# The seam between a normed product and the next sublayer, with its three engines in written order

## The chip, the cores and the metric

The kernel runs on one core of one Trainium2 chip. The metric is the time of one execution in device microseconds (us); several executions of each kernel are compared. The engines are called TensorE (PE), VectorE (DVE), ScalarE (ACT), GpSimd (POOL) and SyncE (SP, which issues the loads).

## What is computed

Two stacks of transformer layers on a sequence of 256 tokens of width 1024, in float32. Each of the two layers of the first stack is a mixer, a cross-attention and an mlp; the second stack, two layers more, has a mixer and a gated feed-forward in each. What matters here is the seam between two sublayers of the first stack: a product, the norm of what it gives, the sum into x, and the norm of the new x, which is what the next product reads.

```python
def rms_norm(x, g):
    xf = x.astype(jnp.float32)
    y = xf * lax.rsqrt(jnp.mean(xf * xf, axis=-1, keepdims=True) + RMS_EPS)
    return (y * g.astype(jnp.float32)).astype(x.dtype)
...
        x = x + rms_norm(merged @ w_mix_out[l], ln_mix_post[l])

        h = rms_norm(x, ln_xa_pre[l])
        mn = rms_norm(mem, ln_mem[l])
        x = x + rms_norm(cross_attention(h, mn, xa_wq[l], xa_wkv[l], xa_wo[l]), ln_xa_post[l])

        h = rms_norm(x, ln_mlp_pre[l])
        x = x + rms_norm(jnp.square(jax.nn.relu(h @ mlp_w1[l])) @ mlp_w2[l], ln_mlp_post[l])
```

## The kernel before

**Layout.** x is held with its 1024 features as eight chunks of 128 partitions by 256 tokens. A weight block of 128 output features is a piece of 128x1024. A product of float32 accuracy is three products of rounded parts: each operand is split into a high part and the rest, and hi·hi, hi·lo and lo·hi are added in PSUM. So a block costs 8 (chunks) x 3 = 24 matmuls of 128x256.

**Weights.** Pieces are loaded by SP into `wraw`. `Weights.make` splits one: ACT copies it into `whi` (L371), DVE subtracts that into `wlo` (L372). There are four buffers of each, and `Weights.get` keeps three pieces made ahead of the one in use.

**The end of a normed product** (`post_units`, `post_evict`, `post_close`). There are three such products in a layer of the first stack: "mo" (the mixer's output), "xo" (the cross-attention's output) and the second product of the mlp. For each of eight output blocks, ACT squares the block out of PSUM (`ysq`, L698), ACT or DVE scales it into `yg` (L701, L703), and DVE adds the squares up in `yacc` (L707). After the last block `inv_rms` takes the mean over features with matmuls of 128x1 (from `yacc` and the last `ysq`), DVE adds epsilon (`st_m`, L461), POOL takes the power -1/2 (`st_tm_y`, L451), and PE spreads the result over the partitions in PSUM (`rp`). Then yg is multiplied by it and added to x: for the first two chunks one by one on DVE (L716, L719), for the next two in one go (L724), for the last four on POOL (L726), from a copy of rp in SBUF that ACT makes (`st_rep_y`, L717).

**The start of the next sublayer.** The new x, times the gain of the next norm, is split into `xgh` (ACT, L508) and `xgl` (DVE, L509), chunk by chunk. The factor 1/rms of this norm is taken out of the product and put in behind it, so the product can start before it is known. For that factor ACT squares x two chunks at a time (`sq_acc`, L493, then `sq_t`, L496, three times, through one buffer), and POOL adds them up (three adds of 128x512, L497, and one of 128x256, L500). `opening` runs the first three blocks of the product side by side, chunk by chunk, since chunk k of x becomes known one after the other. The mean over `sq_acc` stands in PE's order behind these three blocks and a fourth, that is behind 96 matmuls.

**What sets the order.** In the part of the program that is touched here a list scheduler sets the order of the instructions on each engine from its own estimates. Only from a later phase on the code is run with `manual_schedule`, in which PE, ACT and DVE follow the order in which the code is written. POOL and SP are never fixed that way.

Of the kernel before, what the change touches and what calls it, by code (L numbers as in the profile page):

```python
# [307 lines left out]
class Weights:  # L308


    def __init__(self, nc, w, ring, parts, tails, keys, ahead):
        self.nc, self.w, self.ring, self.parts, self.tails = nc, w, ring, parts, tails
        self.subs = []
        off, _ = _offsets()
        for key in keys:
            for i in range(len(off[key][1])):
                self.subs.append((key, i))
        self.ahead = ahead
        self.made, self.used = 0, 0
        self.ready = []  # L320
        self.keys, self.sent, self.loaded = keys, 0, deque()

    def deepen(self, open_pool, n):

# [24 lines left out]
        self.loaded.append(([t[:, j * m : j * m + m] for j in range(n)], tail))  # L349

    def make(self):
        nc = self.nc
# [8 lines left out]
        res = []  # L361
        for tail in range(1 + (subs[i] > 1024)):
            src = self.curt[:, i, :] if tail else self.cur[i]
            pool, bufs, n = (self.tails, 2, 256) if tail else (self.parts, 4, min(subs[i], 1024))
            tag = "t" if tail else "m"
            hi = pool.tile([P, 256 if tail else 1024], F32R, name="whi", tag="whi" + tag, bufs=bufs)
            lo = pool.tile([P, 256 if tail else 1024], F32R, name="wlo", tag="wlo" + tag, bufs=bufs)
            step = n if 0 < self.made < len(self.subs) - 2 else 512
            for g in range(0, n, step):
                c = slice(g, g + step)  # L370
                nc.scalar.activation(hi[:, c], src[:, c], AF.Copy)  # L371
                nc.vector.tensor_sub(lo[:, c], src[:, c], hi[:, c].bitcast(F32))  # L372
            res += [hi, lo]
        self.ready.append((key, i, *res))
        self.made += 1

    def get(self, key, i):
        while self.made < len(self.subs) and self.made <= self.used + self.ahead:
            self.make()
        k, j, *res = self.ready.pop(0)  # L380
        assert (k, j) == (key, i), ((k, j), (key, i))
        self.used += 1
        return res


class Net:
    def __init__(self, tc, io, out, ctx, tap=None, stop=None):
        self.tc, self.nc, self.io, self.out, self.ctx = tc, tc.nc, io, out, ctx
        self.tap = tap or (lambda name, ap: None)
        self.stop = stop  # L390
# [62 lines left out]
    def inv_rms(self, parts, tag):  # L453

        nc = self.nc
        ps = self.bank()
        for h in range(2):
            for i, sq in enumerate(parts):
                self.mm(ps[:, h : h + 1], sq[:, h * P : h * P + P], self.cv("mean"), i == 0, i == len(parts) - 1)
        m = self.keep.tile([P, 2], F32, name="st_m", tag="st_m", bufs=2)  # L460
        nc.vector.tensor_scalar(m, ps[:, 0:2], EPS, None, op0=ALU.add)  # L461
        tm = self.keep.tile([P, 2], F32, name="st_tm_" + tag, tag="st_tm_" + tag)
        self.rsqrt(tm, m, 2)
        return tm
# [79 lines left out]
    def order(self):  # L544

        self.ordered = self.tc.manual_schedule(engines=ORDERED)
        self.ordered.__enter__()

    def run(self, units):

        for u in units:
            if u[0] == "w":
                u[3](*self.ws.get(u[1], u[2]))
            else:
                u[1]()
# [16 lines left out]
    def fm_units(self, key, xh, xl, evict, nblk=2, each=False):  # L572

        st = {}

        def begin(i):
            if i == 0 or each:
                st["ps"] = self.bank("mm")
            return part(i)

        def part(i):
            o = 0 if each else i * S
            return st["ps"][:, o : o + S]
# [7 lines left out]
        def step(i, k, hi, lo):  # L591
            a, b = (xh(), xl()) if callable(xh) else (xh, xl)
            self.lin_k(part(i), hi, lo, a, b, k, k == 0 and i == 0, k == 7, skip_group_check=True)
# [12 lines left out]
    @staticmethod  # L606
    def ramp(units, n=3):

        held, out, count = [], [], 0
        for u in units:  # L610
            if u[0] != "w" or count == n:
                out.append(u)
                continue
            count += 1

            def g(hi, lo, parts=u[3].parts, last=count == n):
                held.append((parts, hi, lo))
                if not last:
                    return
                for (begin, _, _, i), _, _ in held:  # L620
                    begin(i)
                for k in range(8):
                    for (_, step, _, i), h, l in held:
                        step(i, k, h, l)
                for (_, _, end, i), _, _ in held:
                    end(i)

            out.append((*u[:3], g))
        return out

    def opening(self, units, n=3, a=3, held=4, b=4):
# [3 lines left out]
        for u in units:  # L635
# [3 lines left out]
            if count < held:  # L639
                begin, step, end, i = u[3].parts  # L640
                ends.append((end, i))

                def g(hi, lo, p=u[3].parts, at=count):
                    side.append((p, hi, lo))
                    if at < n - 1:
                        return
                    for (begin, _, _, i), _, _ in side:
                        begin(i)
                    for k in range(8):
                        for (_, step, _, i), h, l in side:  # L650
                            step(i, k, h, l)
                    side.clear()

                out[-1] = (*u[:3], g)
            if count == a:
# [25 lines left out]
    def post_units(self, kind, l, xh, xl, gkey, nxt):  # L681
# [2 lines left out]
        units = []  # L684
        for j in range(4):
            units += self.fm_units((kind, l, j), xh, xl, lambda i, ps, j=j: self.post_evict(2 * j + i, ps, gkey, l), each=True)
        units.append(("x", lambda: self.post_close(nxt)))
        return units

    def post_evict(self, n, ps, gkey, l):  # L690
        nc = self.nc
        if n == 0:
            self.yg = self.keep.tile([P, 8, S], F32, name="yg", tag="big")
            self.yacc = self.keep.tile([P, S], F32, name="yacc", tag="sq_acc")
            sq = self.yacc
# [4 lines left out]
        if n % 2 == 0:  # L700
            nc.scalar.activation(self.yg[:, n, :], ps, AF.Copy, scale=g)  # L701
        else:
            nc.vector.tensor_scalar(self.yg[:, n, :], ps, g, None, op0=ALU.mult)  # L703
        if n == 7:
            self.ylast = sq
        elif n > 0:
            nc.vector.tensor_add(self.yacc, self.yacc, sq)  # L707

    def post_close(self, nxt):
        nc = self.nc  # L710
        rp, _ = self.stat([self.yacc, self.ylast], "y", copy=False)
        rep = self.early.tile([P, S], F32, name="st_rep_y", tag="st_rep_y")
        self.prep(nxt)
        yg, x = self.yg, self.x
        for c in range(2):
            nc.vector.tensor_mul(yg[:, c, :], yg[:, c, :], rp)  # L716
        nc.scalar.activation(rep, rp, AF.Copy)  # L717
        for c in range(2):
            nc.vector.tensor_add(x[:, c, :], x[:, c, :], yg[:, c, :])  # L719
        self.prep_pair(0)  # L720
        for j in range(1, 4):
            v = yg[:, 2 * j : 2 * j + 2, :]
            if j == 1:
# [3 lines left out]
        for j in range(1, 4):  # L727
            v, xv = yg[:, 2 * j : 2 * j + 2, :], x[:, 2 * j : 2 * j + 2, :]
            nc.vector.tensor_add(xv, xv, v)
            self.prep_pair(j)  # L730


    def softmax(self, s, nh, n, pool, gate=None, stride=None):
# [95 lines left out]
    def mix_phase(self, l):  # L829
# [7 lines left out]
        def open_c():  # L837
# [6 lines left out]
            nc.gpsimd.memset(st["zr"][:, :, 0:1], 0.0)  # L844
# [841 lines left out]
    def mlp_phase(self, l):  # L1686
# [27 lines left out]
        units += second(14) + second(15)  # L1714

        def close():
            self.post_close(("ln_mix_pre", 1) if l == 0 else ("nmix", 0))
# [49 lines left out]
    def even_phase(self):  # L1767
# [3 lines left out]
        def pre():  # L1771
# [5 lines left out]
            nc.gpsimd.memset(st["xr"][:, :, 0:3], 0.0)  # L1777
# [936 lines left out]
```

## Time and profile before

| what | us |
|---|---|
| runs shown | 2707.53, 2710.4, 2711.75 |
| their median | 2710.4 |
| the profiled execution | 2709.63 |
| its span, first to last instruction | 2707.8 |
| PE busy | 2643.1 (98%) |
| DVE busy | 2068.0 (76%) |
| ACT busy | 1601.1 (59%) |
| POOL busy | 213.5 (8%) |

The span is the part of an execution between its first and its last instruction. An engine's busy time counts its instructions alone, so the span less PE's busy time is the time in which PE did nothing. The granted clock is a share of full speed: 1.00 is 2.4 GHz and 0.50 is 1.2 GHz.

### The profile page before, as it was taken

The numbers are of one execution on the slowest core, as the hardware profiler recorded it, in microseconds if no ns is written. First come the engines' busy times: TensorE is split into PE (matmuls) and PEld (weight loads), VectorE is DVE, ScalarE is ACT, GpSimd is POOL, SyncE is SP. The second block draws the span as 40 slices with busy tenths as digits, with TensorE's granted clock in tenths as the row PEclk, the third lists the DMA queues.
The fourth block names the chain that finished last, engine by engine and source line by source line (L and its number), as shares of the span: only waits on it lengthen the run. The fifth ranks groups of instructions, "written<-read, shape, count | busy, mean of one in ns | idle before, by whom it ended". The sixth has DMA issues, their size and how long they took to land.

```text
span 2707.8 us, 44209 instructions
## 1 busy us (share of the span) xinstructions
PE 2643.1 (98%) x17870; PEld 2405.5 (89%) x17870; DVE 2068.0 (76%) x2527; ACT 1601.1 (59%) x2136; POOL 213.5 (8%) x188
## 2 busy tenths in 40 slices
PE   8999999999999999999999999999999999999998
PEld 7989999998989999998999999778887888788876
DVE  6776756556875765557876677999999999999997
ACT  4434545444533544444654456777777777777776
POOL 1031101001031111001010011000000000000000
PEclk9999999999999999999899999999999999999999
DMA  7423444553322433554375544999899989998991
GB/s 255 138 98 134 156 156 169 185 187 137 133 100 98 179 141 140 180 180 163 118 297 186 179 175 175 354 358 364 321 363 356 365 323 363 354 357 333 359 353 66
DMA packets 99853, 612.70 MB, mean 226 GB/s; under 512 B 10616, under 2 KB 20344, under 8 KB 31928
## 3 DMA queue, kind: packets, MB, share of 16 engines
q1 hardware_dynamic: 99208, 608.74, 60.9%
q8 instruction: 142, 2.33, 0.3%
q0 software_dynamic: 432, 1.06, 0.1%
q14 instruction: 71, 0.58, 0.1%
HBM read 608.17 MB, written 1.06 MB: 225 GB/s over the span
## 4 chain that ended last, share of the span: by engine, by line
PE 49%; DVE 2%; ACT 1%; issue 0%; POOL 0%; ACTq 0%
PE ps_mm L422 32%; PE ps_b L422 16%; PE ps_b L426 1%; DVE wlo L372 1%; ACT whi L371 0%; DVE room L430 0%; DVE mt L2280 0%; DVE acc L2443 0%; DVE room L2126 0%; DVE fv L2632 0%; ACT acc L2538 0%; DVE x L1761 0%; ACT room L2106 0%; PE ps_r L2527 0%; DVE xgl L509 0%
## 5 line engine op out<-in xcount | busy, mean ns | idle before, releaser
L372 DVE TENSOR_TENSOR wlo<-wraw,whi 128x1024 fp32r<-128x1024 f32 (+1 forms) x1129 | 1376.5, 1239 | 383.8 <-ACT whi L371 372.9
L371 ACT ACTIVATE whi<-wraw 128x1024 fp32r<-128x1024 f32 (+1 forms) x1129 | 1177.6, 1055 | 747.6 <-PE ps_mm L422 552.3
L422 PE MATMUL ps_mm<-xgh,whi 128*128 128x256 f32 x2048 | 591.1, 289 | 14.5 <-ACT whi L371 7.7
L422 PE MATMUL ps_mm<-whi,gx 128*128 128x512 f32 x1792 | 591.1, 399 | 0.0
L422 PE MATMUL ps_mm<-xgh,wlo 128*128 128x256 f32 x2048 | 585.0, 286 | 5.1 <-DVE wlo L372 5.1
L422 PE MATMUL ps_mm<-xgl,whi 128*128 128x256 f32 x2048 | 586.0, 286 | 1.8 <-DVE xgl L509 1.8
L422 PEld LDWEIGHTS ps_mm<-xgh,whi 128*128 128x128 f32 x2048 | 393.7, 193 | 20.4 <-ACT xgh L508 8.0
L422 PEld LDWEIGHTS ps_mm<-whi,gx 128*128 128x128 f32 x1792 | 337.4, 188 | 79.3 <-issue 0.5
L422 PEld LDWEIGHTS ps_mm<-xgh,wlo 128*128 128x128 f32 x2048 | 391.7, 191 | 7.0 <-DVE wlo L372 6.7
L422 PEld LDWEIGHTS ps_mm<-xgl,whi 128*128 128x128 f32 x2048 | 392.0, 191 | 4.6 <-DVE xgl L509 3.0
L422 PE MATMUL ps_mm<-wlo,gx 128*128 128x512 f32 x896 | 355.0, 396 | 0.2 <-DVE wlo L372 0.2
L422 PE MATMUL ps_b<-whi,room 128*128 128x512 f32 x896 | 294.6, 397 | 0.0
L422 PEld LDWEIGHTS ps_mm<-wlo,gx 128*128 128x128 f32 x896 | 168.7, 188 | 39.1 <-issue 0.7
L422 PEld LDWEIGHTS ps_b<-whi,room 128*128 128x128 f32 x896 | 168.2, 188 | 39.5 <-issue 0.2
L422 PE MATMUL ps_b<-hl,whi 128*128 128x256 f32 x688 | 194.5, 283 | 0.0
L422 PE MATMUL ps_b<-hh,wlo 128*128 128x256 f32 x688 | 194.4, 283 | 0.0
L422 PE MATMUL ps_b<-hh,whi 128*128 128x256 f32 x688 | 193.8, 283 | 0.0
L422 PE MATMUL ps_b<-wlo,room 128*128 128x512 f32 x448 | 176.8, 395 | 0.0
L422 PEld LDWEIGHTS ps_b<-hh,wlo 128*128 128x128 f32 x688 | 132.0, 192 | 0.0
L422 PEld LDWEIGHTS ps_b<-hl,whi 128*128 128x128 f32 x688 | 131.9, 192 | 0.0
L422 PEld LDWEIGHTS ps_b<-hh,whi 128*128 128x128 f32 x688 | 131.5, 192 | 0.0
L422 PEld LDWEIGHTS ps_b<-wlo,room 128*128 128x128 f32 x448 | 84.2, 188 | 19.4 <-issue 0.2
(544 smaller groups left out, 3628.9 us busy)
## 6 DMA issues: line engine op xcount, KB each, us to landing
wraw<-in_w SPq DMA_DIRECT2D x557, 1024.0 KB, 5.1
wrawt<-in_w SPq DMA_DIRECT2D x32, 256.0 KB, 5.4
wraw<-in_w SPq DMA_DIRECT2D x8, 512.0 KB, 5.1
cmpw<-in_cmpw SPq DMA_DIRECT2D x2, 1024.0 KB, 8.6
mem<-in_memt SPq DMA_DIRECT2D x2, 1024.0 KB, 8.3
wraw<-in_w SPq DMA_DIRECT2D x2, 560.0 KB, 4.8
x<-in_xt SPq DMA_DIRECT2D x4, 256.0 KB, 5.3
c_rd<-in_cst SPq DMA_DIRECT2D x2, 512.0 KB, 6.9
```

What stands on the lines that cost most here:

```text
L371: nc.scalar.activation(hi[:, c], src[:, c], AF.Copy)
L372: nc.vector.tensor_sub(lo[:, c], src[:, c], hi[:, c].bitcast(F32))
L422: self.nc.tensor.matmul(out, lhsT, rhs, start=start, stop=stop, **kw)
L426: self.nc.tensor.transpose(out, in_, self.ident[:k, :k])
```

## The change

- `fix` and `free` are new: between them the instructions of PE, ACT and DVE keep the order in which the code is written. `fix` is called ahead of the last block of "xo" in both layers, and ahead of the last part of the mlp's second product (there with `hold`, which stops weights from being made ahead); `free` is called when the three opening blocks of the next sublayer have been issued. That makes four seams: xo to mlp, twice, mlp to the mixer of layer 1, and mlp to the second stack. The "mo" seams run the new code without being fixed.
- `Weights.make` is cut in two, so that the copy on ACT and the subtraction on DVE can be written at different places. `post_close` issues the copies of the pieces that are missing to three ahead (one at xo, two at the mlp), then the mean, one subtraction, the spread, and the other subtraction at the very end.
- In `post_close` the first two chunks are written as multiply, add, xgh for each in turn, with the copy of rp on ACT between the two xgh; both xgl follow.
- `inv_rms` runs the two halves of `yacc` first and then those of `ysq`.
- The side-by-side blocks run, in each chunk, hi·xh of all three, then lo·xh of all three, then hi·xl of all three, where each block had its three in a row. This holds for every opening and ramp that is written with these functions.
- Of the scalings of `yg`, ACT has blocks 0, 2, 4 and 5, DVE the others. Two fills with zero move from POOL to DVE.

```diff
+    def fix(self, hold=False):
+        self.ws.held = hold
+        self.fixed = self.tc.manual_schedule(engines=ORDERED)
+        self.fixed.__enter__()
+
+    def free(self):
+        if self.fixed:
+            self.fixed.__exit__(None, None, None)
+        self.fixed, self.ws.held = None, False
...
-        for h in range(2):
-            for i, sq in enumerate(parts):
-                self.mm(ps[:, h : h + 1], sq[:, h * P : h * P + P], self.cv("mean"), i == 0, i == len(parts) - 1)
+        for i, sq in enumerate(parts):
+            for h in range(2):
+                a, z = i == 0 and h == 0, i == len(parts) - 1
+                self.mm(ps[:, h : h + 1], sq[:, h * P : h * P + P], self.cv("mean"), a, z, skip_group_check=True)
...
                     for k in range(8):
-                        for (_, step, _, i), h, l in side:
-                            step(i, k, h, l)
+                        for m in range(3):
+                            for (_, step, _, i), h, l in side:
+                                step(i, k, h, l, m)
                     side.clear()
+                    self.free()
...
     def post_close(self, nxt):
         nc = self.nc
-        rp, _ = self.stat([self.yacc, self.ylast], "y", copy=False)
+        los = []
+        if self.fixed:
+            self.ws.held = True
+            while self.ws.made <= self.ws.used + 3:
+                los.append(self.ws.make_hi())
+        tm = self.inv_rms([self.yacc, self.ylast], "y")
+        if los:
+            los.pop(0)()
+        rp, _ = self.spread(tm, "y", copy=False)
...
         for c in range(2):
             nc.vector.tensor_mul(yg[:, c, :], yg[:, c, :], rp)
-        nc.scalar.activation(rep, rp, AF.Copy)
+            nc.vector.tensor_add(x[:, c, :], x[:, c, :], yg[:, c, :])
+            g = self.pv(nxt, c)
+            nc.scalar.activation(self.nh[:, c, :], x[:, c, :], AF.Copy, scale=g)
+            if c == 0:
+                nc.scalar.activation(rep, rp, AF.Copy)
         for c in range(2):
-            nc.vector.tensor_add(x[:, c, :], x[:, c, :], yg[:, c, :])
-        self.prep_pair(0)
+            g = self.pv(nxt, c)
+            nc.vector.scalar_tensor_tensor(
+                self.nl[:, c, :], x[:, c, :], g, self.nh[:, c, :].bitcast(F32), op0=ALU.mult, op1=ALU.subtract
+            )
...
             self.prep_pair(j)
+        for f in los:
+            f()
```

What stands on DVE at the first xo seam (cross-attention of layer 0 to its mlp), from the mean on; the names in brackets are the semaphores that an instruction waits for. Before:

```order
L461 TENSOR_SCALAR st_m<-ps_b 128x2 [waits PE_49]
L716 TENSOR_TENSOR yg<-yg,ps_b 128x256 [waits PE_49]
L716 TENSOR_TENSOR yg<-yg,ps_b 128x256
L719 TENSOR_TENSOR x<-x,yg 128x256 [waits DVE_49] x2
L724 TENSOR_TENSOR yg<-yg,ps_b 128x512 [waits Activation_49]
L509 SCALAR_TENSOR_TENSOR xgl<-x,prm,xgh 128x256 [waits Activation_49] x2
L729 TENSOR_TENSOR x<-x,yg 128x512 [waits DVE_49]
L729 TENSOR_TENSOR x<-x,yg 128x512 [waits Pool_49] x2
L509 SCALAR_TENSOR_TENSOR xgl<-x,prm,xgh 128x256 [waits Activation_49] x6
```

The same place on DVE after:

```order
L469 TENSOR_SCALAR st_m<-ps_b 128x2 [waits PE_49]
L381 TENSOR_TENSOR wlo<-wraw,whi 128x1024 [waits Activation_49]
L751 TENSOR_TENSOR yg<-yg,ps_b 128x256 [waits PE_49]
L752 TENSOR_TENSOR x<-x,yg 128x256 [waits DVE_49]
L751 TENSOR_TENSOR yg<-yg,ps_b 128x256 [waits Activation_49]
L752 TENSOR_TENSOR x<-x,yg 128x256 [waits DVE_49]
L759 SCALAR_TENSOR_TENSOR xgl<-x,prm,xgh 128x256
L759 SCALAR_TENSOR_TENSOR xgl<-x,prm,xgh 128x256 [waits Activation_49]
L765 TENSOR_TENSOR yg<-yg,ps_b 128x512
L770 TENSOR_TENSOR x<-x,yg 128x512 [waits DVE_49]
L517 SCALAR_TENSOR_TENSOR xgl<-x,prm,xgh 128x256 [waits Activation_49] x2
L770 TENSOR_TENSOR x<-x,yg 128x512 [waits Pool_49]
```

The subtraction for a weight stands behind the mean, the second multiply by rp waits for ACT and stands behind the first add, and the later adds and xgl alternate (the last row shown is followed by two xgl, one more add and two xgl more).

ACT at the same seam, from the last square of the old product on. Before:

```order
L371 ACTIVATE whi<-wraw 128x1024
L698 ACTIVATE ysq<-ps_mm 128x256
L717 ACTIVATE st_rep_y<-ps_b 128x256
L508 ACTIVATE xgh<-x,prm 128x256 x2
L493 ACTIVATE sq_acc<-x 128x512
L508 ACTIVATE xgh<-x,prm 128x256 x6
L496 ACTIVATE sq_t<-x 128x512 x3
L371 ACTIVATE whi<-wraw 128x1024 x5
```

The same place on ACT after:

```order
L724 ACTIVATE ysq<-ps_mm 128x256 x2
L376 ACTIVATE whi<-wraw 128x1024
L754 ACTIVATE xgh<-x,prm 128x256
L756 ACTIVATE st_rep_y<-ps_b 128x256
L754 ACTIVATE xgh<-x,prm 128x256
L516 ACTIVATE xgh<-x,prm 128x256 x6
L501 ACTIVATE sq_acc<-x 128x512
L504 ACTIVATE sq_t<-x 128x512 x2
L376 ACTIVATE whi<-wraw 128x1024
L504 ACTIVATE sq_t<-x 128x512
```

The weight's copy has changed places with the last square of the product, the copy of rp with the first xgh, and the first squares of the new x stand behind all eight xgh.

PE at the same seam, from the means on. After:

```order
L429 MATMUL ps_b<-t_ident,yacc 128x1 x2
L429 MATMUL ps_b<-t_ident,ysq 128x1 x2
L429 MATMUL ps_b<-t_ident,st_tm_y 128x128 x2
L429 MATMUL ps_mm<-xgh,whi 128x256 x3
L429 MATMUL ps_mm<-xgh,wlo 128x256 x3
L429 MATMUL ps_mm<-xgl,whi 128x256 x3
```

The three last rows come eight times, where before the three kinds alternated one by one; then follow the 24 matmuls of the fourth block and the mean over `sq_acc`, as before.

## Rows read from the trace of the kernel before

**Rows 1.** The page: span, and busy time of PE's two parts and the other engines.

```profile
span 2707.8 us, 44209 instructions
...
PE 2643.1 (98%) x17870; PEld 2405.5 (89%) x17870; DVE 2068.0 (76%) x2527; ACT 1601.1 (59%) x2136; POOL 213.5 (8%) x188
```

**Rows 2.** PE's waits, whole span: us in total, times, longest us.

```profile
PE ps_b L422 <- POOL st_tm_y L451: 7.4, 4, 2.3
PE ps_mm L422 <- DVE wlo L372: 7.3, 10, 1.1
PE ps_mm L422 <- ACT xgh L508: 6.9, 4, 1.7
```

**Rows 3.** Two stretches: length, busy us (instructions) of each engine, PEclk, DMA, GB/s.

```profile
434.30:441.25 6.95, 4.79 (x19) 4.20 (x20) 5.85 (x10) 2.65 (x7) 2.69 (x2) 0.51 0.77 301
441.25:451.00 9.75, 9.75 (x81) 9.66 (x81) 4.88 (x9) 6.26 (x10) 5.71 (x4) 1.00 0.01 2
```

**Rows 4.** Timeline of PE, first xo seam: start, length, instruction, [idle before, and releaser].

```profile
430.62 0.29 PE L422 MATMUL ps_b<-t_ident,yacc 128*128 128x1 f32 x2
...
432.08 0.38 PE L422 MATMUL ps_b<-t_ident,ysq 128*128 128x1 f32 x2 [1.17 <-ACT ysq L698]
...
451.15 0.50 PE L422 MATMUL ps_b<-t_ident,sq_acc 128*128 128x1 f32 x4
```

**Rows 5.** Timeline of DVE, same seam.

```profile
431.79 1.22 DVE L372 TENSOR_TENSOR wlo<-wraw,whi 128x1024 fp32r<-128x1024 f32 x1 [1.31 <-ACT whi L371]
...
435.40 0.75 DVE L716 TENSOR_TENSOR yg<-yg,ps_b 128x256 f32<-128x256 f32 x2 [1.93 <-PE ps_b L422]
...
436.74 0.68 DVE L724 TENSOR_TENSOR yg<-yg,ps_b 128x512 f32<-128x512 f32 x1
437.33 2.34 DVE L509 SCALAR_TENSOR_TENSOR xgl<-x,prm,xgh 128x256 fp32r<-128x256 f32 x2
439.60 1.88 DVE L729 TENSOR_TENSOR x<-x,yg 128x512 f32<-128x512 f32 x3
441.40 2.45 DVE L509 SCALAR_TENSOR_TENSOR xgl<-x,prm,xgh 128x256 fp32r<-128x256 f32 x6
```

**Rows 6.** Timeline of ACT, same seam.

```profile
430.70 1.06 ACT L371 ACTIVATE whi<-wraw 128x1024 fp32r<-128x1024 f32 x1 [1.18 <-PE ps_mm L422]
431.66 0.37 ACT L698 ACTIVATE ysq<-ps_mm 128x256 f32<-128x256 f32 x1
436.24 0.38 ACT L717 ACTIVATE st_rep_y<-ps_b 128x256 f32<-128x256 f32 x1 [4.21 <-DVE yg L716]
...
440.31 2.51 ACT L508 ACTIVATE xgh<-x,prm 128x256 fp32r<-128x256 f32 x6 [2.36 <-DVE x L729]
442.72 0.62 ACT L496 ACTIVATE sq_t<-x 128x512 f32<-128x512 f32 x1
```

**Rows 7.** Timeline of POOL, same seam.

```profile
433.55 0.69 POOL L451 TENSOR_TENSOR st_tm_y<-st_m,t_ident 128x2 f32<-128x2 f32 x1 [2.40 <-DVE st_m L461]
436.70 2.69 POOL L726 TENSOR_TENSOR yg<-yg,st_rep_y 128x512 f32<-128x512 f32 x2 [2.46 <-ACT st_rep_y L717]
443.47 1.52 POOL L497 TENSOR_TENSOR sq_acc<-sq_acc,sq_t 128x512 f32<-128x512 f32 x1 [4.08 <-issue]
...
449.15 1.60 POOL L500 TENSOR_TENSOR sq_acc<-sq_acc 128x256 f32<-128x256 f32 x1
```

**Rows 8.** Timeline of all engines at the mlp seam of layer 0, three rows of it.

```profile
627.90 1.60 POOL L451 TENSOR_TENSOR st_tm_y<-st_m,t_ident 128x2 f32<-128x2 f32 x1 [2.32 <-DVE st_m L461]
...
630.82 0.75 DVE L716 TENSOR_TENSOR yg<-yg,ps_b 128x256 f32<-128x256 f32 x2 [1.87 <-PE ps_b L422]
...
647.56 0.50 PE L422 MATMUL ps_b<-t_ident,sq_acc 128*128 128x1 f32 x4
```

**Rows 9.** The tile sq_acc on POOL, whole span: duration ns min/median/max, first and last start.

```profile
L497 POOL TENSOR_TENSOR sq_acc<-sq_acc,sq_t x36: 1280/1392/2100, 11.6 to 1683.6; 128x512 f32<-128x512 f32 x36
L500 POOL TENSOR_TENSOR sq_acc<-sq_acc x12: 737/1202/1655, 17.3 to 1685.0; 128x256 f32<-128x256 f32 x12
```

More of the change, by code (lines that the diff above doesn't have):

```diff
@@ L321, in __init__ @@
         self.keys, self.sent, self.loaded = keys, 0, deque()
+        self.held = False
     def deepen(self, open_pool, n):
@@ L351, in make, with make_hi @@
     def make(self):
+        self.make_hi()()
+    def make_hi(self):
         nc = self.nc
@@ L360, in make @@
                 self.load()
-        res = []
+        res, los = [], []
         for tail in range(1 + (subs[i] > 1024)):
@@ L371, in make @@
                 nc.scalar.activation(hi[:, c], src[:, c], AF.Copy)
-                nc.vector.tensor_sub(lo[:, c], src[:, c], hi[:, c].bitcast(F32))
+                los.append((lo[:, c], src[:, c], hi[:, c].bitcast(F32)))
             res += [hi, lo]
@@ L375, in make @@
         self.made += 1
+        return lambda: [nc.vector.tensor_sub(*a) for a in los]
     def get(self, key, i):
-        while self.made < len(self.subs) and self.made <= self.used + self.ahead:
+        while self.made < len(self.subs) and self.made <= self.used + (0 if self.held else self.ahead):
             self.make()
@@ L389, in __init__ @@
         self.tap = tap or (lambda name, ap: None)
+        self.fixed = None
         self.stop = stop
@@ L589, in end, with step @@
                 evict(st["ps"][:, : nblk * S])
-        def step(i, k, hi, lo):
+        def step(i, k, hi, lo, n):
             a, b = (xh(), xl()) if callable(xh) else (xh, xl)
-            self.lin_k(part(i), hi, lo, a, b, k, k == 0 and i == 0, k == 7, skip_group_check=True)
+            w = (hi, lo, hi)[n][:, k * P : k * P + P]
+            self.mm(part(i), w, (a, a, b)[n][:, k, :], k == n == 0 and i == 0, k == 7 and n == 2, skip_group_check=True)
         def f(i):
@@ L622, in g @@
                 for k in range(8):
-                    for (_, step, _, i), h, l in held:
-                        step(i, k, h, l)
+                    for n in range(3):
+                        for (_, step, _, i), h, l in held:
+                            step(i, k, h, l, n)
                 for (_, _, end, i), _, _ in held:
@@ L649, in g @@
                     for k in range(8):
-                        for (_, step, _, i), h, l in side:
-                            step(i, k, h, l)
+                        for m in range(3):
+                            for (_, step, _, i), h, l in side:
+                                step(i, k, h, l, m)
                     side.clear()
+                    self.free()
                 out[-1] = (*u[:3], g)
@@ L686, in post_units @@
             units += self.fm_units((kind, l, j), xh, xl, lambda i, ps, j=j: self.post_evict(2 * j + i, ps, gkey, l), each=True)
+        if kind == "xo":
+            units.insert(-1, ("x", self.fix))
         units.append(("x", lambda: self.post_close(nxt)))
@@ L694, in post_evict @@
             self.yacc = self.keep.tile([P, S], F32, name="yacc", tag="sq_acc")
+            self.ycount = 0
             sq = self.yacc
@@ L699, in post_evict @@
         g = self.pv((gkey, l), n)
-        if n % 2 == 0:
+        if n > 0 and n < 7:
+            nc.vector.tensor_add(self.yacc, self.yacc, sq)
+        if self.ycount in (0, 2, 4, 5):
             nc.scalar.activation(self.yg[:, n, :], ps, AF.Copy, scale=g)
@@ L705, in post_evict @@
             self.ylast = sq
-        elif n > 0:
-            nc.vector.tensor_add(self.yacc, self.yacc, sq)
+        self.ycount += 1
     def post_close(self, nxt):
         nc = self.nc
-        rp, _ = self.stat([self.yacc, self.ylast], "y", copy=False)
+        los = []
[7 more added lines that the diff above has]
+        rp, _ = self.spread(tm, "y", copy=False)
         rep = self.early.tile([P, S], F32, name="st_rep_y", tag="st_rep_y")
@@ L843, in open_c @@
             st["zr"] = c.tile([P, 7, S + 1], F32, name="zr")
-            nc.gpsimd.memset(st["zr"][:, :, 0:1], 0.0)
+            nc.vector.memset(st["zr"][:, :, 0:1], 0.0)
             for m in range(4):
@@ L1713, in mlp_phase @@
             units += (m1[j] if j > 2 else []) + second(j - 2)
-        units += second(14) + second(15)
+        end = second(15)
+        units += second(14) + end[:1] + [("x", lambda: self.fix(True))] + end[1:]
         def close():
@@ L1776, in pre @@
             st["xr"] = p.tile([P, 4, S + 3], F32, name="xr")
-            nc.gpsimd.memset(st["xr"][:, :, 0:3], 0.0)
+            nc.vector.memset(st["xr"][:, :, 0:3], 0.0)
             for n in ("yr", "q", "k"):
```

## The prediction

> **What bounds the kernel now.** I read the page first: TensorE (PE) is busy for 2643.1 of 2707.8 us [rows 1], so the whole program holds some 65 us in which PE does nothing, and a change of order can win no more than its share of these. The second view is the list of PE's waits [rows 2]. Its line for the power on GpSimd (POOL) that ends a normed product (four waits, 7.4 us) and the line for xgh (four, 6.9) belong to the seams that the change rewrites. The third view is the table of stretches at one seam, from the cross-attention product of layer 0 to the mlp [rows 3]: in the 6.95 us after the power PE is granted half its clock (0.51, the 1.2 GHz level) and is busy for 4.79; in the 9.75 us behind that it has the full clock and issues 81 matmuls without a gap, 0.12 each. Last come the timelines of the four engines at this seam [rows 4 to 7] and three rows of the next seam, mlp to mix [rows 8].
>
> One seam, read through. The last product matmul starts 0.12 before the first mean, thus at 430.50. VectorE (DVE) begins yg*rp at 435.40 [rows 5]; I call this moment rp and split the seam there. In front of it lie the squares of the last block, the mean, the power and its spread. Behind it lie 96 matmuls of the next product (three opening blocks and one more, 24 each), and then, as the next thing in PE's order, the mean over the squares of the new x. This mean starts at 451.15 [rows 4], that is rp + 15.75. It can't start before POOL's last add ends, at 449.15 + 1.60 = 450.75 [rows 7], and it starts 0.4 behind it: PE and POOL arrive at nearly the same time now. 96 matmuls at the full-clock pitch of 0.12 would take 11.5; the seam takes 20.65 from 430.50, so some 9 us are lost here. There are four such seams: xo0 (this one), xo1, mlp0 and mlp1, two after xo and two after the mlp's second product.
>
> **Front part, before rp: a gain.** Before, ScalarE (ACT) runs a weight split (whi) at 430.70 and ysq only at 431.66 [rows 6]; PE waits 1.17 for it [rows 4]. After, ysq stands ahead of whi and can start about 0.9 sooner (ysq 0.34 to 0.71 behind the last product matmul), and one mean pass fewer stands behind it (0.2). Against this, wlo, which needs that whi, now falls right on the power: whi (1.06) runs behind ysq until 1.7, wlo (1.22) until 2.9. Before, wlo was over by 433.01 [rows 5], and the power at 433.55 took 0.69 [rows 7]. Where wlo did lie on the power, at mlp0, the power took 1.60 [rows 8]. If the power comes first it ends at 2.3, and with the 1.15 of the spread between power and yg*rp (434.24 to 435.40) rp is at 3.45, where it is at 4.90 now: 1.45 sooner. If wlo comes first the power ends some 0.55 behind it, at 3.45, and rp is at 4.6: 0.3 sooner. I take 0.9, halfway, at each of the two xo seams. At mlp0 and mlp1 the power is the long one already; there I take 1.0 and 0.7, from ysq and the shorter mean. Sum of the front: -3.5 (bounds -1.9 and -4.9).
>
> The Trainium skill bears on this choice (SBUF — State Buffer, section "SBUF: two separate sides"): VectorE operations with two SBUF inputs and GpSimd operations share a port pair, held whole by whichever starts first. The 1.60 agrees with it, the start decides; by the rule with wlo first, both xo terms would be 0.3 and the front -2.3.
>
> **Back part, behind rp: a loss.** I walk the new order with durations of the old. Before, DVE did both multiplies and both adds of the first pair, then the third multiply, while ACT made rep (436.24) for POOL; POOL's two yg multiplies (2.69 from 436.70 [rows 7]) then blocked only xgl, whose two took 2.34 [rows 5] where six others took 2.45, 0.41 each. The next three adds ended at 441.48.
> After, in us from rp: first multiply 0.4, its add 0.8, xgh0 (0.42 to 0.5) 1.3, then rep (0.38 [rows 6]) 1.7. The second multiply waits for rep: the two read the same PSUM tile one engine at a time, as rep did before for yg*rp (4.21 of idle put down to it [rows 6]), and rep stands first now: 2.15. POOL starts its two multiplies at 1.75 and ends at 3.0 and 4.4. The second add, two SBUF operands, is now caught by the first of them (3.3), xgl0 by the second (4.7). Then, unhindered: xgl1 5.1, third multiply 5.7 (0.68), add 6.4 (0.63, a third of 1.88 [rows 5]), xgh2 6.95. From here on an add and two xgl alternate, with an xgh between: adds at 8.5 and 10.5, xgh7 at 11.4. Before, xgh7 ended at 440.31 + 2.51 = 442.82, rp + 7.4 [rows 6].
> The squares are the point. Before, the first stood ahead of xgh2, the second started right behind xgh7, at 442.72, and POOL's chain ran from 443.47 to 450.75, 7.28 us. After, the first two stand behind xgh7: 0.6 + 0.5 more, so POOL's first add starts at rp + 12.5. With the chain as long as before (7.28) it ends at 19.8. The bounds: of the 7.28 POOL was busy for 5.71 [rows 3], so 1.57 were waits for the one square buffer; with these, three adds of 1.28 and a final of 0.74 [rows 9] make 6.15, so 18.65; with wlo's beside each, up to 20.2. The mean starts 0.4 behind, at 19.0 to 20.6; I take the middle, 19.8.
> PE itself gets there sooner: its first nine matmuls stop at xgl0 (4.7), the third k waits for xgh2 (6.95), the last for xgl7 (11.9); then 24 more at 0.12 to 0.21 and the backlog: 16.5 to 18.5. So it waits for POOL some 2 us, which it never does now, and half clock before that is hidden by this wait.
> Loss per seam: xo0 19.8 - 15.75 = 4.05; mlp0 with mean at 647.56 and rp at 630.82 [rows 8] stands at 16.74 now, 3.06; xo1 and mlp1 I take as xo0, 4.05 each, and 0.5 more at mlp1, where small decay operations slip in between. Together +15.7.
>
> **The rest.** The mo to xa seams get the new order of the same code without being fixed: their multiplies and adds wait on rep too, the opening comes some 0.5 later, and one wlo wait of up to 1.1 [rows 2] may go: +0.5 each. The opening at the start of the program, +0.3. The block-by-block order of hi and lo products elsewhere, and the two small fills given to DVE, beside other work: 0, bounds ±1. Instruction counts are otherwise equal, and the order of loads on SP is the same but for one half load.
>
> **Sum.** -3.5 + 15.7 + 1.3 = +13.5. The profiled execution took 2709.63; that gives 2723.1. The median of the runs is 2710.4, 0.8 above; **2724**.
>
> **Rivals.**
> (B) The blocks on the port are milder. If DVE gets in ahead of POOL at the second add and xgl0, its work from 1.7 is 6.7 long, xgh7 ends at 8.5 to 9, POOL's chain at 16 to 17, the mean at 17.4: +1.65 three times and +0.66, 5.6 in all; 5.6 - 3.5 + 1.3 = +3.4, **2714**. For it: what starts first is a matter of 0.1 us. Against: xgl0 and xgl1 were both caught at this seam.
> (C) The clock falls again. Before, the stretch at half clock starts inside the long gap and lasts 6.95 us [rows 3], hidden in part. After, PE has several gaps before the mean and a new one of 2 us at it. If half clock then lasts as long behind the mean, where PE is the bound, each seam pays half of 6.95, 3.4; three seams, +10: **2734**. The Trainium skill (TensorE: Matmul & The Clock Gate, section "What's actually happening") says that the slow level is the default and activity lifts it, which is for this; the trace has no 2 us gap of this kind to show it.
> (D) Faster. The mechanism would be POOL's chain at its shortest: DVE unhindered, chain 6.15 from 9.6, mean at 16.1 (+0.35 three times, -0.6 at mlp0: +0.4); front at its best, -4.9; both wlo waits at mo gone, -2.1. 2709.6 - 6.6 + 0.8 = **2704**. The point: from POOL's last add before rp + 16 on. Against: the squares were moved behind xgh7, and even then nothing of the back part is won.
> (E) The order does not move what I think, since the waits set it anyway: 2710. The listings speak against it.
>
> **Chances.** Forecast 0.55 (its own range 2717 to 2731), B 0.17, C 0.18, D 0.06, E 0.04. One can tell about 0.2% from no change here, 5.4 us. D is faster; E and most of B fall within; the rest is slower: faster 0.06, same 0.17, slower 0.77. The range, 2710 to 2738, holds the forecast, C and most of B, with the bounds of the back part (four times ±0.8) on top.
>
> **What would show it.** In the profile after: PE waiting for POOL sq_acc, four times, 1 to 3 us each; PE's wait for ysq gone or under 0.5; xgh7 about 11 us after yg*rp; the second add on DVE over 1 us long; the power at xo 0.7 (front right at its best) or about 1.6. I am wrong if the mean over sq_acc starts under 17 us after rp, or if PE still comes to it last.

## The result

The changed kernel takes 2729.39 us in the median of four runs (2727.39 to 2732.42), the kernel before 2711.07 (2707.53 to 2715.33); the ratio is 1.0071, 95% interval 1.0056 to 1.0086. It is slower by some 18 to 19 us. The forecast was 2724, slower, and the measured time lies in its range.

The profiled executions differ by 19.5 us in span (2707.8 and 2727.4). First PE's waits, over the whole span (us in total, times, longest us), to be laid beside [rows 2]:

```profile
PE ps_b L429 <- POOL sq_acc L508: 10.4, 4, 3.0
...
PE ps_mm L429 <- DVE wlo L381: 7.4, 9, 1.3
PE ps_mm L429 <- DVE xgl L759: 7.2, 4, 2.2
PE ps_mm L429 <- ACT xgh L754: 6.0, 4, 1.5
PE ps_b L429 <- POOL st_tm_y L458: 6.0, 4, 2.0
```

Two more lines of the kernel before, for comparison:

```profile
PE ps_b L422 <- ACT ysq L698: 2.3, 2, 1.2
...
PE ps_mm L422 <- DVE xgl L509: 1.8, 4, 0.5
```

The first line of the new list has no counterpart in the old one: at each of the four seams PE stands before the mean of the next norm and waits for POOL's last add. The wait for the first xgl has come up with it, to 1.8 us per seam from 0.45. The line for the power has fallen from 7.4 to 6.0, and ysq is gone from the list.

The xo seam of layer 0 on PE (start, length, instruction, idle before and what ended it), for [rows 4]:

```profile
432.64 0.52 PE L429 MATMUL ps_b<-t_ident,yacc 128*128 128x1 f32 x4
433.28 0.60 PE L429 MATMUL ps_b<-t_ident,ysq 128*128 128x1 f32 x4
...
437.13 1.01 PE L429 MATMUL ps_mm<-xgh,whi 128*128 128x256 f32 x3 [1.51 <-ACT xgh L754]
...
440.45 0.80 PE L429 MATMUL ps_mm<-xgl,whi 128*128 128x256 f32 x2 [1.67 <-DVE xgl L759]
...
456.20 0.68 PE L429 MATMUL ps_b<-t_ident,sq_acc 128*128 128x1 f32 x4 [2.10 <-POOL sq_acc L508]
```

DVE at the same seam, for [rows 5]:

```profile
434.20 1.23 DVE L381 TENSOR_TENSOR wlo<-wraw,whi 128x1024 fp32r<-128x1024 f32 x1
435.66 0.42 DVE L751 TENSOR_TENSOR yg<-yg,ps_b 128x256 f32<-128x256 f32 x1 [0.23 <-PE ps_b L429]
...
437.38 0.42 DVE L751 TENSOR_TENSOR yg<-yg,ps_b 128x256 f32<-128x256 f32 x1 [0.84 <-ACT st_rep_y L756]
437.84 1.16 DVE L752 TENSOR_TENSOR x<-x,yg 128x256 f32<-128x256 f32 x1
438.92 1.87 DVE L759 SCALAR_TENSOR_TENSOR xgl<-x,prm,xgh 128x256 fp32r<-128x256 f32 x2
...
446.82 0.88 DVE L517 SCALAR_TENSOR_TENSOR xgl<-x,prm,xgh 128x256 fp32r<-128x256 f32 x2 [0.58 <-ACT xgh L516]
```

The second multiply waits 0.84 for rep, the second add takes 1.16 where the first takes 0.42, and before each later pair of xgl DVE stands idle for 0.58 until ACT has the xgh.

ACT and POOL at the same seam, for [rows 6, 7]:

```profile
432.84 0.38 ACT L724 ACTIVATE ysq<-ps_mm 128x256 f32<-128x256 f32 x1 [1.67 <-PE ps_mm L429]
...
446.28 0.91 ACT L516 ACTIVATE xgh<-x,prm 128x256 fp32r<-128x256 f32 x2 [1.16 <-DVE x L770]
447.10 0.61 ACT L501 ACTIVATE sq_acc<-x 128x512 f32<-128x512 f32 x1
447.62 0.62 ACT L504 ACTIVATE sq_t<-x 128x512 f32<-128x512 f32 x1
```

```profile
434.16 0.70 POOL L458 TENSOR_TENSOR st_tm_y<-st_m,t_ident 128x2 f32<-128x2 f32 x1 [0.98 <-DVE st_m L469]
437.43 2.69 POOL L767 TENSOR_TENSOR yg<-yg,st_rep_y 128x512 f32<-128x512 f32 x2 [2.57 <-ACT st_rep_y L756]
448.37 1.29 POOL L505 TENSOR_TENSOR sq_acc<-sq_acc,sq_t 128x512 f32<-128x512 f32 x1 [8.25 <-issue]
...
454.56 1.59 POOL L508 TENSOR_TENSOR sq_acc<-sq_acc 128x256 f32<-128x256 f32 x1
457.38 1.62 POOL L458 TENSOR_TENSOR st_tm_x<-st_m,t_ident 128x2 f32<-128x2 f32 x1 [1.23 <-DVE st_m L469]
```

The eighth xgh ends at 447.19, both first squares stand behind it, POOL sits idle for 8.25 us and starts its first add 12.7 us behind yg*rp (435.66), where it was 8.1 before. Its last add ends at 456.15, and PE starts the mean 0.05 later.

With each seam cut at yg*rp and at the mean, as the prediction cuts it, and the way on to the first spread of the next norm (st_tm_x) as a third part, the timelines give this (us; before, after):

| seam | last product matmul to yg*rp | yg*rp to mean | mean to spread | sum |
|---|---|---|---|---|
| xo0 | 4.90, 3.14 | 15.75, 20.54 | 3.64, 4.93 | 24.29, 28.61 |
| mlp0 | 5.69, 4.77 | 16.74, 20.31 | 3.32, 4.92 | 25.76, 30.00 |
| xo1 | 4.55, 3.14 | 16.01, 19.95 | 3.44, 3.42 | 24.00, 26.52 |
| mlp1 | 5.39, 4.77 | 15.75, 20.51 | 4.42, 4.79 | 25.56, 30.06 |
| change | -4.72 | +17.06 | +3.24 | +15.58 |

The first column runs from the start of the last product matmul. At the mlp seams that is not 0.12 before the first mean: PE stands in between and waits for the sum in yacc, 0.66 us before and 0.22 after.

So 15.6 of the 19.5 us lie in the four seams. The two mo seams, cut the same way, add 2.85 (0.69 and 2.16). The remaining 1.1 is a balance of parts between -1.8 and +1.4 that hold none of these seams.

The third column is mostly the clock. Two stretches of the changed kernel from the mean to the spread, xo0 and xo1 (length, busy us with instructions by engine, granted clock, DMA):

```profile
456.20:461.20 5.00, 5.00 (x29) 5.00 (x30) 2.23 (x3) 0.00 (x0) 1.62 (x1) 0.66 0.84 303
1088.70:1092.20 3.50, 3.44 (x29) 3.45 (x30) 2.28 (x3) 0.00 (x0) 1.62 (x2) 1.00 0.88 297
```

The same 29 recorded matmuls take 5.00 us where PE is granted 0.66 of its clock (the 1.2 GHz level for part of the stretch) and 3.50 where it has all of it. The fall comes behind three of the four waits for sq_acc, and not behind the one at xo1, which is 2.26 us long and no shorter than the 2.10 at xo0.

### The profile page after: what moved, and what is told of

It reads as the page before. It is cut to its first block, busy times and chain, and to the rows that moved or that the text cites. A ratio compares the mean times of both kernels' runs of the same rounds, so it can differ in the third digit from the quotient of the medians.

```text
span 2727.4 us, 44218 instructions
## 1 busy us (share of the span) xinstructions
PE 2651.9 (97%) x17870; PEld 2414.3 (89%) x17870; DVE 2069.8 (76%) x2530; ACT 1601.1 (59%) x2136; POOL 217.1 (8%) x185
## 3 DMA queue, kind: packets, MB, share of 16 engines
q0 software_dynamic: 432, 1.06, 0.1%
HBM read 608.17 MB, written 1.06 MB: 223 GB/s over the span
## 4 chain that ended last, share of the span: by engine, by line
PE 86%; DVE 6%; issue 4%; ACT 2%; POOL 2%; DMA 0%; SPq 0%; DVEq 0%; ACTq 0%; POOLq 0%
PE ps_mm L429 55%; PE ps_b L429 29%; DVE wlo L381 2%; PE ps_b L433 2%; ACT whi L376 1%; POOL sq_acc L505 1%; DVE xgl L517 0%; DVE x L752 0%; DMA mem<-in_memt 0%; ACT sq_t L504 0%; POOL sq_acc L508 0%; DVE ml L517 0%; DVE ab L1439 0%; DVE room L437 0%; DVE mt L2324 0%
## 5 line engine op out<-in xcount | busy, mean ns | idle before, releaser
L429 PE MATMUL ps_mm<-xgh,whi 128*128 128x256 f32 x2048 | 576.4, 292 | 14.8 <-ACT whi L376 7.5
L429 PE MATMUL ps_mm<-xgh,wlo 128*128 128x256 f32 x2048 | 569.4, 288 | 7.3 <-DVE wlo L381 7.2
L429 PE MATMUL ps_mm<-xgl,whi 128*128 128x256 f32 x2048 | 568.7, 288 | 7.2 <-DVE xgl L759 7.2
L429 PEld LDWEIGHTS ps_mm<-xgl,whi 128*128 128x128 f32 x2048 | 386.2, 193 | 10.0 <-DVE xgl L759 8.4
```

The source lines that it names most:

```text
L429: self.nc.tensor.matmul(out, lhsT, rhs, start=start, stop=stop, **kw)
```

## The experiments

The theory is that of the prediction: with the new order the xgh and xgl come later, the squares stand behind the last of them, and so POOL's adds end when PE has long been done. All kernels below start from the changed one.

**Giving the fixed order up behind the spread** (e1). The front and the matmul order of the opening stay.

```diff
         rp, _ = self.spread(tm, "y", copy=False)
+        self.free()
...
         for c in range(2):
             nc.vector.tensor_mul(yg[:, c, :], yg[:, c, :], rp)
+        nc.scalar.activation(rep, rp, AF.Copy)
+        for c in range(2):
             nc.vector.tensor_add(x[:, c, :], x[:, c, :], yg[:, c, :])
...
+        self.prep_pair(0)
```

> The changed kernel, with the fixed order given up right behind the spread of 1/rms, and the old code behind it (multiply, multiply, rep, add, add, then the chunks), so that the scheduler again sets what stands behind yg*rp: squares of the first pair ahead of the third xgh, all adds ahead of the later xgl. The front (squares ahead of the weight copy, short mean) and the new order of the opening's matmuls stay. Theory (the loss lies in the order of DVE and ACT behind yg*rp): each of the four seams keeps its 0.2 to 1.8 us of the front and loses the 3.6 to 4.8 us of the back, the mo seams lose nothing; 2707 to 2710 us, and PE waits for POOL sq_acc no more than before. Rival (the opening's new order of matmuls is what costs): the back stays long, above 2720.

Measured: 2709.27 us beside 2709.17 for the kernel before, ratio 0.9994 (0.998 to 1.0008; it is not the quotient of the two medians). PE's wait for sq_acc is down from 10.4 us to 0.7, in two waits. The profiled execution is the fastest of its ten (2700.74). At xo0 POOL's last add, and PE's mean 15.8 us behind yg*rp (434.02):

```profile
447.76 0.74 POOL L508 TENSOR_TENSOR sq_acc<-sq_acc 128x256 f32<-128x256 f32 x1
...
449.82 0.50 PE L429 MATMUL ps_b<-t_ident,sq_acc 128*128 128x1 f32 x4
```

The whole loss lies in the written order behind the spread; e7 below keeps that part fixed and shows that it is what DVE and ACT do there. The opening's matmul order, which is still the new one here, isn't the cause.

**Squares early** (e2): the new order with one thing moved.

```diff
+        self.squares(x, 0)
         for j in range(1, 4):
...
             self.prep_pair(j)
+            self.sqx = self.squares(x, j)
```

> The changed kernel, with one thing moved: the squares of each pair of chunks, and POOL's adds of them, are written right behind that pair's xgh and xgl, no longer behind the eighth xgh. Theory (the squares' place sets when the mean can start): POOL's last add ends at 16 to 17.5 us behind yg*rp where it ends at 20 to 20.5 now, though POOL's adds now catch some adds and xgl of DVE on the way; PE's wait for sq_acc falls from 2.6 to under 1 us per seam, and with it goes the half clock behind the mean; 2713 to 2719 us. Rival (DVE's chain through xgl7 is the bound, the squares only its symptom): the wait moves from sq_acc to xgl, 2725 to 2730.

Measured: 2710.12 us, 1.0007 (0.9998 to 1.0017), a little better than the theory had it. At xo0 DVE, ACT, POOL and PE:

```profile
446.85 1.25 DVE L517 SCALAR_TENSOR_TENSOR xgl<-x,prm,xgh 128x256 fp32r<-128x256 f32 x2 [0.58 <-ACT xgh L516]
...
442.62 0.61 ACT L504 ACTIVATE sq_t<-x 128x512 f32<-128x512 f32 x1
...
449.53 0.74 POOL L508 TENSOR_TENSOR sq_acc<-sq_acc 128x256 f32<-128x256 f32 x1
...
452.54 0.50 PE L429 MATMUL ps_b<-t_ident,sq_acc 128*128 128x1 f32 x4
```

The last xgl ends no earlier than in the changed kernel: 448.10, 12.8 us behind yg*rp (435.32), even 0.7 later, since POOL's early adds catch it. But POOL is done at 450.27, and PE comes to the mean at 452.54 (17.2) without waiting for it. From the mean to the spread it takes 3.3 to 4.0 us, so the clock's share is gone with the wait. With the late xgl alone the kernel is as fast as before, within the interval; but the gain of the front is in this time too, and the four seams sum to 101.5 us in its profile, where e1 has 95.7. The rival, that DVE's chain is the bound and the squares only its symptom, falls.

**The first pair as before** (e3): multiply, multiply, rep, add, add, xgh, xgh, and all the rest as changed, the squares late.

```diff
         for c in range(2):
             nc.vector.tensor_mul(yg[:, c, :], yg[:, c, :], rp)
+        nc.scalar.activation(rep, rp, AF.Copy)
+        for c in range(2):
             nc.vector.tensor_add(x[:, c, :], x[:, c, :], yg[:, c, :])
...
-            if c == 0:
-                nc.scalar.activation(rep, rp, AF.Copy)
```

> The changed kernel, with the first pair written as before: multiply, multiply, rep, add, add, xgh, xgh; all the rest of the new order stays, the squares behind the eighth xgh too. Theory: the second add is no longer caught by POOL, DVE's chain moves up by some 0.8 us per seam, and the mean with it, 3 us in all, and the mo seams get 2 to 3 back: 2723 to 2725 us. Rival (the swap of rep and the second multiply is the main loss): two thirds of the loss go, under 2717.

Measured: 2728.61 us, 1.0068 (1.0046 to 1.0089). The local step is what the theory said: xgh7 ends 10.7 us behind yg*rp instead of 11.5, and the mean starts at 19.1 to 19.6 instead of 20 to 20.5. The median shows none of the 3 us that were expected, though four runs (2722.96 to 2729.67) can't rule them out: the interval holds 2723 to 2725 too. What follows is read from the profiled execution (2729.03). PE's wait, and two stretches from the mean to the spread (mlp0 and xo1):

```profile
PE ps_b L429 <- POOL sq_acc L508: 13.1, 4, 3.6
```

```profile
655.60:661.70 6.10, 6.08 (x29) 6.08 (x30) 1.54 (x4) 0.00 (x0) 1.14 (x1) 0.52 0.90 344
1088.20:1094.50 6.30, 6.21 (x29) 6.21 (x30) 2.40 (x3) 0.05 (x1) 1.65 (x2) 0.50 0.85 320
```

PE's own work moved up by more than POOL's, so the wait grew from 10.4 to 13.1, and behind it the clock stayed low longer: in the profiled execution the way from the mean to the spread takes 6.0 and 6.1 us at these two seams, where the changed kernel has 4.9 and 3.4. At xo0 it is the other way round: 3.4 for 4.9, with the full clock behind a wait of 2.55. Over the four seams the mean comes 4.0 us sooner and the way on is 2.5 longer. The mo seams, expected to get 2 to 3 back, each had a half-clock stretch of 3.4 us and stood 1.9 above the kernel before. In this execution the clock took most of what the order gained.

**The old matmul order** in side-by-side blocks (e4). The same swap is made in the ramp, the other place where blocks run side by side; it is left out here and under e5 and e8.

```diff
-                        for m in range(3):
-                            for (_, step, _, i), h, l in side:
-                                step(i, k, h, l, m)
+                        for (_, step, _, i), h, l in side:
+                            for m in range(3):
+                                step(i, k, h, l, m)
```

> The changed kernel, with the matmuls of blocks side by side in the old order, block by block (hi xh, lo xh, hi xl) in each chunk. Theory: PE waits for POOL's adds at the end of each seam whatever it did before, so nothing changes at the four seams; 2728 to 2730 us, half-clock stretches aside. Rival (six matmuls in a row that need no xgl, instead of two, help or hurt): a gain or loss of over 4 us.

Measured: 2730.43 us, 1.0082 (1.0063 to 1.0101), 0.4 above the theory's range and with no gain or loss of the rival's size. PE's waits:

```profile
PE ps_mm L429 <- DVE xgl L759: 10.0, 4, 2.5
PE ps_b L429 <- POOL sq_acc L508: 8.1, 4, 2.7
```

Block by block PE stops for xgl after fewer matmuls, so that wait is longer (10.0 for 7.2) and the one behind it shorter (8.1 for 10.4): their sum moves by half a microsecond. At these seams the order of the matmuls only decides where PE waits.

**The old work of DVE, the squares late** (e7): the fourth corner, for the question whether the squares' place does it alone. The third multiply and POOL's two also stand ahead of the first xgl again; everything stays in fixed order.

```diff
         for c in range(2):
             nc.vector.tensor_mul(yg[:, c, :], yg[:, c, :], rp)
+        nc.scalar.activation(rep, rp, AF.Copy)
+        for c in range(2):
             nc.vector.tensor_add(x[:, c, :], x[:, c, :], yg[:, c, :])
...
         for j in range(1, 4):
-            v, xv = yg[:, 2 * j : 2 * j + 2, :], x[:, 2 * j : 2 * j + 2, :]
-            nc.vector.tensor_add(xv, xv, v)
+            nc.vector.tensor_add(x[:, 2 * j : 2 * j + 2, :], x[:, 2 * j : 2 * j + 2, :], yg[:, 2 * j : 2 * j + 2, :])
+        for j in range(1, 4):
             self.prep_pair(j)
```

> The changed kernel with the fixed order kept to the end of the opening, but DVE and the xgh of ACT written as they stood before (multiply, multiply, add, add, third multiply, two xgl, three adds, six xgl); only the squares stay behind the eighth xgh, as the change has them. Theory (two delays add: late xgh and squares behind them): xgh7 ends at 7.5 behind yg*rp, POOL's first add starts at 8.7, its last ends at 15.2 to 17, the mean starts at 16 to 17; 2708 to 2714 us. Rival (the place of the squares is the whole cause by itself): the mean stays near 20, 2722 to 2730.

Measured: 2709.14 us, 0.9999 (0.9989 to 1.0009). ACT, POOL and PE at xo0, with yg*rp at 436.24:

```profile
441.17 2.51 ACT L516 ACTIVATE xgh<-x,prm 128x256 fp32r<-128x256 f32 x6 [2.90 <-DVE x L770]
443.59 0.61 ACT L501 ACTIVATE sq_acc<-x 128x512 f32<-128x512 f32 x1
...
450.28 1.79 POOL L508 TENSOR_TENSOR sq_acc<-sq_acc 128x256 f32<-128x256 f32 x1
...
452.13 0.61 PE L429 MATMUL ps_b<-t_ident,sq_acc 128*128 128x1 f32 x4
```

The squares stand behind the eighth xgh as in the changed kernel, but that one ends at 443.68, 7.4 us behind yg*rp, and the mean starts at 15.9. Nothing is lost. Set beside e3, this also tells what makes xgh7 late: of 4.1 us the first pair's order is 0.85 (11.5 to 10.7), and the rest (10.7 to 7.4) comes from the third multiply, POOL's two and the later adds standing behind xgl. So the four corners are (medians, and the mean's start behind yg*rp at the four seams):

| | squares early | squares behind xgh7 |
|---|---|---|
| DVE and xgh as before | e1: 2709.3; 15.4 to 16.6 | e7: 2709.1; 15.7 to 16.5 |
| DVE and xgh in the new order | e2: 2710.1; 17.2 to 18.8 | changed: 2729.4; 20.0 to 20.5 |

The corner of e1 is placed by the scheduler behind the spread, the others are fixed. The late squares alone cost nothing. The late DVE and xgh alone start the mean 1.4 to 3.0 us later than in e1; in time that is 1 to 4 us by the medians and the ratios, which the intervals can't tell from nothing. The two in a row cost some 19 us.

**Nothing fixed** (e6): the changed code, placed by the scheduler.

```diff
     def fix(self, hold=False):
-        self.ws.held = hold
-        self.fixed = self.tc.manual_schedule(engines=ORDERED)
-        self.fixed.__enter__()
+        self.fixed = None
```

> The changed kernel with nothing fixed: the scheduler places the new code on all engines. Its order has the squares of each pair behind that pair's xgh, and the weight copy ahead of the last square of the product again. Theory: the loss goes with the fixed order, since the squares are early again; the front's gain goes too but for the shorter mean; mean 16 to 18 us behind yg*rp, 2709 to 2715 us. Rival (the new code is slow in any order, by rep behind xgh): above 2720.

Measured: 2715.11 us, 1.0023 (1.0014 to 1.0033), just above what was expected. The mean starts at 16.2 to 17.4, so the main loss is gone with the fixed order. The front is nearly as slow as before (4.55 to 5.39). In the profiled execution the four seams sum to 100.6 us, 1.0 more than before, and each mo seam takes 2.2 more, with a half-clock stretch of 3.4 us in it. Together that is 5.3 us, near the 6 of the medians; but this execution is the fastest of its ten (2710.36) and other parts of it are shorter, so where the 6 us lie is not shown.

**The front alone** (e5): e1 with the old matmul order.

```diff
+        self.free()
...
-                        for m in range(3):
-                            for (_, step, _, i), h, l in side:
+                        for (_, step, _, i), h, l in side:
+                            for m in range(3):
```

> The front alone, once more with the fixed order given up behind the spread and the old code behind it, and now also with the matmuls of side-by-side blocks in the old order (block by block). Of the change there remain the squares of the last block ahead of the weight copy, the short mean, and the scalings of yg. Theory: the four seams keep 1.1 to 1.7 us each, and the half us that the new matmul order costs at the start and at each mo seam is gone; 2703 to 2708 us. Rival (the gain in front is given back behind the mean, or to the clock): 2708 to 2712, no difference from before.

Measured: 2706.27 us beside 2709.2, 0.9989 (0.998 to 0.9999), eleven runs. The four seams sum to 96.2 us in its profiled execution, where the kernel before has 99.6 and the changed one 115.2. It is the only one of eight whose interval lies below 1, and that by a hair, so that it is faster is likely but not shown.

**Three parts together** (e8): the first pair as before, squares early, old matmul order, that is the edits of e3, e2 and e4.

```diff
+        nc.scalar.activation(rep, rp, AF.Copy)
...
+        self.squares(x, 0)
...
+            self.sqx = self.squares(x, j)
...
+                        for (_, step, _, i), h, l in side:
+                            for m in range(3):
```

> Three things put together: the first pair as before (multiply, multiply, rep, add, add, xgh, xgh), the squares of each pair right behind its xgh and xgl, and the old order of matmuls in side-by-side blocks; the front and the alternating adds and xgl stay. Theory: xgh7 ends at 10 to 11 us, POOL's adds at 15 to 16, the mean starts at 16 to 17.5, and the mo seams lose nothing: 2704 to 2709 us, at best a little under the kernel before. Rival (POOL's early adds catch so many adds and xgl that PE waits for xgl instead): 2711 to 2716.

Measured: 2708.26 us, 0.9993 (0.9984 to 1.0003), within what was expected. The mean starts at 16.5 to 18.1, at mlp1 later than forecast, and each mo seam takes 0.8 more than before. No other version is under e5.

## Why the prediction was right, and where it was off

**The step that carries it, right.** The order of the code became the order of the engines, and the chain was walked as it ran: at xo0 the predicted and measured times behind yg*rp are 1.3 and 1.42 for xgh0, 3.3 and 3.34 for the end of the second add, 4.7 and 4.7 for xgl0, 11.4 and 11.5 for xgh7, 12.5 and 12.7 for POOL's first add, 19.8 and 20.5 for its last. The forecast wait for sq_acc is there four times, 2.1 to 3.0 us each. That squares and late xgh act together was in the walk, but the text says that the squares are the point; e7 shows that their place alone costs nothing, and e2 that the late xgh and xgl alone cost little.

**Back part, too small by 1.4 in 17.** The prediction found POOL's last add at 19.8 and the mean 0.4 behind it, thus 20.2, but took the middle of its bounds, 19.8. Measured are 19.95 to 20.54: the mean starts 0.05 behind POOL, not 0.4, since PE is already standing there, and the last add itself ran beside a wlo (1.59 for the 0.74 that it can take).

**Front, too small by 1.2.** Taken were -0.9 at each xo seam and -1.0 and -0.7 at the mlp ones; measured -1.76, -1.41, -0.92 and -0.62, together -4.72 for the -3.5 of the forecast. The miss is the halfway choice at xo: the power started 0.04 us ahead of wlo (434.16 and 434.20) and took 0.70, the best case. At xo0 0.35 came on top that the case did not have: from the power's end to yg*rp it took 0.80 for 1.15, with the clock granted in full, where before it was 0.61 there. At mlp0 the power started 0.96 sooner (2.78 to 1.82 behind the last product matmul) and was as long as before, 1.63, with wlo started ahead of it. So the mlp terms are right in size, but not by ysq and the shorter mean alone. Of the 0.96, the mean starts 0.45 sooner: PE's wait for yacc is 0.22 for 0.66, since the changed code adds to yacc ahead of the scaling of yg, which the list of changes leaves out. The mean is 0.15 shorter. And st_m starts 0.04 behind it for 0.41, since DVE is no longer busy with a wlo and a scaling at that moment. The bounds given, -1.9 and -4.9, do not follow from the prediction's cases either, which give -2.3 and -4.6.

**Behind the mean, left out of the sum.** Rival C, priced at 3.4 per seam, came at three of four seams with 1.3, 1.6 and 0.4 in the difference, +3.2 in all. It was given 0.18 as a case of its own and 0 in the forecast, so a part of it that was likely enough was missing. The length of the wait alone does not tell whether it comes: the clock fell behind a wait of 1.63 us (e4, xo1) and held behind one of 2.55 (e3, xo0). The Trainium skill's statement (TensorE: Matmul & The Clock Gate, section "What's actually happening"), that activity lifts the slow level and the slow one is the default, agrees with the 0.66 behind the wait at xo0; why it held through the wait at xo1 no run here shows.

**The mo seams: 0.5 each was forecast, 0.69 and 2.16 measured, by another step.** The multiplies and adds that wait on rep cost PE nothing here, since a product that does not read x stands in between. One wait for wlo of 1.07 us did go, and PE begins the opening 1.04 sooner (14.22 behind yg*rp for 15.26). But the opening takes 1.7 longer: at mo0 it waits 0.55 for xk, and 1.05 and 1.29 for wlo, where before it waited 0.38 and 1.06 for wlo. The second seam has a half-clock stretch of 3.4 us on top. e6 has 2.2 at both.

**The sum.** In the profiled execution the parts are -4.7 (front), +17.1 (back), +3.2 (behind the mean), +2.8 (mo) and +1.1 (the rest), 19.5 for the 13.5 of the forecast. The 6 us that are missing lie behind the mean (3.2), in the mo seams (1.9), the back (1.4) and the rest (0.8); the front went the other way (-1.2). The measured time lies in the range, and the direction and the main term came about as walked; the total of 2724 was 5 us short.

**Rival B** (the port is milder) fell: the second add was caught (1.16 us for 0.42). **Rival D** fell with it. What the front gains, the runs put at 0 to 3 us (e1 0.9994, e5 0.9989, e7 0.9999, e8 0.9993). The four seams of e1, e5 and e7 show 3.5 to 3.9 in the profiled executions, and their mo seams give 0.7 to 2.2 of that back; in one execution, parts without a seam move by as much, so this stays only roughly known.

## What to carry to other kernels

When an order is written by hand, walk every side chain that ends at a later wait, here the squares for the next norm, and not only the chain that starts the next product: a delay that is free alone can be free no longer behind another one. A gap on TensorE of two or three microseconds can cost more than half as much again in the clock behind it (here 1.3 behind 2.1 and 1.6 behind 3.0), and then an earlier start in front of the gap can give less than it seems. When a fixed order costs time, freeing one part of it at a time, and building the four corners of two suspects, finds the pair that does it.

## What the hardware showed that was not expected

The power on POOL (128x2, 0.70 us) and wlo on DVE (1.22 us) met in both orders. The timeline of the changed kernel at mlp0, for [rows 8]:

```profile
633.14 1.23 DVE L381 TENSOR_TENSOR wlo<-wraw,whi 128x1024 fp32r<-128x1024 f32 x1
633.29 1.63 POOL L458 TENSOR_TENSOR st_tm_y<-st_m,t_ident 128x2 f32<-128x2 f32 x1 [174.29 <-DVE st_m L469]
```

With wlo ahead by 0.15 us, the power took 1.63, ending 0.55 behind wlo. With the power ahead by 0.04 us (xo0, and the same at xo1), neither was any longer: 0.70 and 1.23. The profile's times on POOL are rough, so which of the two was really first by 0.04 is not sure; in either case neither held the other. POOL's 128x512 multiply did hold DVE: the second add took 1.16 for 0.42 and ended 0.28 behind it. So a small operation of POOL that starts first, as the profile has it, did not hold DVE here; the Trainium skill (SBUF — State Buffer, section "SBUF: two separate sides") has the one that starts first keep the ports for its whole length, which fits the large operations and not this one.
